# The numerators of a cached attention cross partitions by sixteen on-chip copies instead of by way of DRAM

## The chip, the cores and the metric

The kernel runs on one core of a Trainium2 chip. The metric is the device time of one execution in microseconds (us); lower is better. The five engines of the core work from queues of their own: TensorE (PE; its weight loads are PEld), VectorE (DVE), ScalarE (ACT), GpSimd (POOL) and SyncE (SP), which here issues nearly all DMAs. They wait for one another through semaphores.

## The reference, cut to what matters

One inference step of a small hybrid decoder: a recurrent layer, then a layer of "forgetting attention" in which each score carries a bias from a running sum of log forget values. It is done for a prompt of 2048 new tokens and, with the same weights, for 8 sample sequences of 8 new tokens each, which attend to 4096 cached positions in 32 pages of 128 rows. Model width 1024, 16 heads of 64.

```python
def fox_block(q, k, v, cq, ck, q_pos, k_pos):
    s = jnp.einsum('bqhd,bkhd->bhqk', q, k).astype(jnp.float32) * (HEAD_DIM ** -0.5)
    s = s + jnp.swapaxes(cq, 1, 2)[:, :, :, None] - jnp.swapaxes(ck, 1, 2)[:, :, None, :]
    mask = k_pos[None, :] <= q_pos[:, None]
    s = jnp.where(mask[None, None], s, -jnp.inf)
    p = jax.nn.softmax(s, axis=-1)
    return jnp.einsum('bhqk,bkhd->bqhd', p.astype(v.dtype), v)
...
    past_k = cache_k[page_table].reshape(Bs, past_len, N_HEADS, HEAD_DIM)
    past_v = cache_v[page_table].reshape(Bs, past_len, N_HEADS, HEAD_DIM)
```

All arithmetic is float32.

## The kernel before

The prompt's work (projections, the recurrence, the attention of 2048 tokens) is one long stream for TensorE. Beside it runs the cached attention of the samples, a generator `decode` that is advanced a step at a time. Its unit is a *turn*: one of 8 sequences and one of two groups of 8 heads, so 16 turns. Turns 0 and 1 run early, beside the first projections, one step after the other. Turns 2 to 15 run beside the second half of the projections and the prompt's attention, and there `period` overlaps three turns: the last products of the previous one, the softmax of this one and the scores of the next.

A turn goes like this:

- `pages` (L1074) loads the turn's 32 pages of keys, four pages of 256 KB into one tile `raw`; `V.transpose` (L1159) turns them into `ktr` in blocks of 32 by 32.
- `scores` (L1127) multiplies them with the queries. VectorE subtracts the result and the prefix sums `sc` of the log forget values from one another into `sc` (L106). `sc` is loaded once a turn from DRAM (L1116, 1 MB) and has one buffer. `new_scores` (L1142) does the same for the 8 new keys; both use one PSUM bank, `dS`.
- `softmax` finds the maxima, and ScalarE makes the numerators in `sc` in place. TensorE sums them (`dsum`, L1205).
- Eight transposes of blocks (L1212) bring the numerators to `sy`. They transpose within groups of 32 partitions only. What is still in the way is that the group of partitions (called i) and a block along the free axis (a) have to change places: 4 groups by 4 blocks, each 32 partitions by 512 values.
- This exchange goes through a DRAM scratch `pd`, one of two: four writes of 256 KB (L1217), one per group i, and one read of 1 MB into `sx` (L1218), which waits for the four writes. `sx` has one buffer; the turn's products read it until its end.
- `values` loads the 32 pages of values through the same four buffers of `raw`, and `products` (L1237) multiplies them with `sx` into `dO`. Then comes the result (L1265).

`sy` is taken from the buffers of `raw` in turns 2 to 15.

The order of the instructions on each engine is not written by hand alone: the program is built with a scheduler that plans all five engines from the dependences and its own estimates of durations, and the order that it finds is what the engines execute. A change of a few DMAs can move instructions everywhere behind it. On SP all DMAs stand in one line. In the compiled program they take eight semaphores in turn, and a DMA waits on its semaphore for the DMA eight before it to land (where another wait does not already make that sure), so that about eight are in flight.

Of the kernel before, what the change touches and what calls it, by code (L numbers as in the profile page):

```python
# [85 lines left out]
def tile_hawk_fox(  # L86
# [8 lines left out]
    V, A, G, T, S = nc.vector, nc.scalar, nc.gpsimd, nc.tensor, nc.sync  # L95
# [9 lines left out]
    def tt(eng, out, a, b, op):  # L105
        eng.tensor_tensor(out, a, b, op=op)  # L106
# [47 lines left out]
    def dt_(name, shape):  # L154
        return dram.tile(shape, F32, name=name, tag=name)
# [15 lines left out]
    qs_d = dt_("qsd", [DB, 32, 4, KB, DS])  # L171


    pd_d = [dt_(f"pd{i}", [4, 32, 4, 512]) for i in range(2)]

    c_d = dt_("cd", [2, 4, 4, DB, NPG // 4, 256])
    cn_d = dt_("cnd", [H, NSAMP])
# [846 lines left out]
    def decode(es, turns, nraw, nktr, ahead):  # L1024
# [28 lines left out]
        def bank(name, tag="d"):  # L1053
            return psum["dec"].tile([P, 512], F32, name=name, tag=tag, bufs=1)

        def spare():
            if ahead:
                return pool.tile([P, 2048], F32, name="sy", tag="raw", bufs=nraw)
            return pool.tile([P, 4096], F32, name="sy", tag="ktr", bufs=nktr)[:, :2048]

        def pages(cache, b, hg, g):

            with ExitStack() as order:

                if len(last) >= 3:
                    order.enter_context(tc.issue_after(last[-3]))
                regs = nc.values_load_multi_w_load_instructions(
                    pt1[0:1, b * NPG + g * 4:b * NPG + g * 4 + 4], engines=[SP], min_val=0, max_val=NPOOL - 1,
                    skip_runtime_bounds_check_because="the table was held between the first page and the last")[1]
            raw = pool.tile([P, 4, 512], F32, name="raw", tag="raw", bufs=nraw)  # L1070
            came = []
            for i in range(4):
                page = cache[ds(regs[i], 1), :, hg * 8:(hg + 1) * 8, :]
                d = S.dma_start(raw[:, i, :], page.rearrange("o k h d -> (o k) (h d)"))  # L1074
                came.append(d)
            last.append(d.ins)
            return raw, came
# [7 lines left out]
        def fetch_q(b):  # L1085
            qb = qbs[b] = pool.tile([P, 4, KB, DS], F32, name="qb", tag="qb")
            for a in range(4):
                S.dma_start(qb[a * 32:(a + 1) * 32], qs_d[b])

        def place_q(b, hg, pr):  # L1090

            G.tensor_tensor(  # L1092
                qw[:, pr].rearrange("p x (m q) -> p x m q", m=4),
                qbs[b][:, :, hg * 4 + pr, :].unsqueeze(2).to_broadcast([P, 4, 4, DS]),
                amask[:, :].unsqueeze(1).unsqueeze(3).to_broadcast([P, 4, 4, DS]), op=ALU.mult)
# [71 lines left out]
        def softmax(t):  # L1167

            dl = t.dl
            b, hg, gmx = t.b, t.hg, t.gmx  # L1170
            if not ahead:
                t.raws = [pages(cache_v, b, hg, x) for x in range(2)]
            while dl.q:
                dl.tick()
                yield HOP

            V.tensor_reduce(mx[:, :8], gmx[:, :, :].rearrange("p g h -> p h g"), axis=AX.X, op=ALU.max)
            mp = bank("dm")
            T.transpose(mp[:, :P], mx[:, :], ident[:, :])
            m1 = pool.tile([8, DS], F32, name="dm1", tag="dm1")  # L1180
            V.tensor_reduce(m1[:, :], mp[:8, :P].rearrange("h (a q) -> h q a", q=DS), axis=AX.X, op=ALU.max)
            V.tensor_scalar(mr[:8, :, :], m1[:, :].unsqueeze(1).to_broadcast([8, 16, DS]), -1.0, 0.0, op0=ALU.mult, op1=ALU.add)
            T.matmul(mp[:, P:P + 8], mr[:, :, :].rearrange("h a q -> h (a q)"), ident[:, :8], start=True, stop=True)
            nm = pool.tile([P, 8], F32, name="dnm", tag="dnm")
            V.tensor_copy(nm[:, :], mp[:, P:P + 8])
            if t.next and t.next[1] == 0:
                fetch_q(t.next[0])
            yield 3 * HOP

            ss = pool.tile([P, 2, 8], F32, name="dss", tag="dss")  # L1190
            tt(V, t.cn[:, :, :], t.cn[:, :, :], nm[:DS, :].unsqueeze(2).to_broadcast([DS, 8, DS]), ALU.add)
            A.activation(pn[:DS, :, :DS], t.cn[:, :, :], AF.Exp)
            V.tensor_reduce(ss[:DS, 1, :], pn[:DS, :, :DS], axis=AX.X, op=ALU.add)
            for j in range(4):
                for h in (2 * j, 2 * j + 1):
                    A.activation(t.sc[:, :, h, :], t.sc[:, :, h, :], AF.Exp, bias=nm[:, h:h + 1], accum_out=ss[:, 0, h:h + 1])
                if t.next:
                    place_q(*t.next, j)
                yield HOP
            tt(V, ss[:DS, 0, :], ss[:DS, 0, :], ss[:DS, 1, :], ALU.add)  # L1200
            dg = pool.tile([P, 8, DS], F32, name="ddg", tag="ddg")
            tt(V, dg[:, :, :], ss[:, 0, :].unsqueeze(2).to_broadcast([P, 8, DS]),
               qmask[:, :].unsqueeze(1).to_broadcast([P, 8, DS]), ALU.mult)
            sp = bank("dsum")
            T.matmul(sp[:, :64], ones[:, :], dg[:, :, :].rearrange("p h q -> p (h q)"), start=True, stop=True)  # L1205
            rb = t.rb = pool.tile([P, 64], F32, name="drb", tag="drb", bufs=2)
            V.reciprocal(rb[:, :], sp[:, :64])


            sy = spare()[:, :].rearrange("p (a x h q) -> p a x h q", a=4, x=8, h=8)  # L1210
            for h in range(8):
                V.transpose(sy[:, :, :, h, :].rearrange("p a x q -> p x a q"), t.sc[:, :, h, :])  # L1212

            sx = pool.tile([P, 4, 8, 8, DS], F32, name="sx", tag="sx")
            pd = pd_d[(b * 2 + hg) % 2]
            for i in range(4):
                S.dma_start(pd[:, :, i].rearrange("a l f -> l a f"), sy[i * 32:(i + 1) * 32].rearrange("p a x h q -> p a (x h q)"))  # L1217
            S.dma_start(sx[:, :, :, :, :].rearrange("p i x h q -> p (i x h q)"), pd.rearrange("a l i f -> (a l) (i f)"))  # L1218
            pt = pool.tile([32, 8, 32], F32, name="dpt", tag="dpt")
            V.transpose(pt[:, :, :].rearrange("p h x -> p (h x)"), pn[:, :, :].rearrange("p h x -> p (h x)"))  # L1220
            pc = t.pc = pcs[(b * 2 + hg) % 2]
            A.copy(pc[:32, :].rearrange("p (h q) -> p h q", h=8), pt[:, :, :DS])
            t.sx = sx
# [49 lines left out]
        def period(p, t, n):  # L1273


            chain_ = softmax(t)
            if n:
                begin(n)
            for who, x in (("v", 5), ("k", 0), ("v", 6), ("k", 1), ("v", 7), ("k", 2), ("k", 3), ("v", 0), ("k", 4),
                           ("v", 1), ("k", 5), ("v", 2), ("k", 6), ("v", 3), ("k", 7), ("v", 4)):  # L1280
                if (who, x) == ("v", 0):
                    yield from chain_
                if who == "k" and n:
                    yield from keys(n, [x])
                elif who == "v" and (t if x < 5 else p):
                    yield from values(t if x < 5 else p, [x])
                if x > 4 or who == "k" and x < 4:
                    yield from islice(chain_, 2)
# [7 lines left out]
        if ahead:  # L1296
            for p, t, n in zip([None] + ts, ts, ts[1:] + [None]):
                yield from period(p, t, n)
            yield from values(ts[-1], [5, 6, 7])
        else:  # L1300
            for t, n in zip(ts, ts[1:] + [None]):
                yield from softmax(t)
                yield from values(t, range(8))
                if n:
                    begin(n)
                    yield from keys(n, range(8))
# [532 lines left out]
```

## Time and profile before

| | |
|---|---|
| median of 3 runs | 3090.09 us (3083.68, 3090.09, 3090.77) |
| profiled execution, span | 3081.2 us (first to last instruction) |
| what lies around the span | 8.9 us, median less span; no time of its own is listed for the profiled execution |
| mean granted clock of TensorE | 0.965 |
| DMA packets, bytes | 492855, 653.25 MB |

The span of a profile runs from the first to the last instruction of one execution; the time of a run also has what the device does before and after. Names such as `sx<-pd` say what an instruction or DMA writes and reads, buffer numbers left out. A row of waits has the engine and line that waited, what ended the wait, the sum in us, the number of waits and the longest. A row in order of time has start, duration (of several merged instructions from the first to the last) and, where there is one, the idle time before in brackets. A row of a tile's instructions has their least, median and greatest duration in ns and the first and last start. A row of windows has the stretch, its length, busy us and instructions of PE, PEld, DVE, ACT and POOL, TensorE's granted clock, the DMA engines' share and GB/s.

### The profile page before, as it was taken

What the parts mean: (1) busy time and instruction counts of PE and PEld (TensorE: products, weight loads), DVE (VectorE), ACT (ScalarE), POOL (GpSimd) and SP (SyncE); (2) the same over time, 40 slices, a digit from 0 to 9 for tenths busy, and PEclk for the clock granted to TensorE, in tenths of its full rate; (3) what the DMA queues carried; (4) which work ended last, traced back from release to release, by engine and by line L of the source; (5) the groups of instructions that cost most, each with busy time, mean ns of one, the idle gap of its engine ahead of it and who ended that gap; (6) DMA issues with size and microseconds to landing.
All of it is one profiled execution on the core that took longest, in us unless ns stands there. A gap on an engine that the chain in (4) does not pass through costs nothing.

```text
span 3081.2 us, 58151 instructions
## 1 busy us (share of the span) xinstructions
PE 2825.8 (92%) x20462; PEld 2177.5 (71%) x20462; DVE 1805.6 (59%) x4012; ACT 1295.0 (42%) x2874; POOL 1155.5 (38%) x1263
## 2 busy tenths in 40 slices
PE   6998999998999989997999799899999988999798
PEld 5997888988999978885797455455545554544587
DVE  7876555424367756755655666666667665543244
ACT  4665432232346655333333334444444445455211
POOL 1663101000025532000001456655656648788322
PEclk9999999999999999998999799999999999999899
DMA  4224547788622266999999998989999996331343
GB/s 121 89 76 150 154 137 216 242 267 254 198 84 86 79 195 198 327 305 315 325 331 307 292 303 261 289 268 321 289 294 314 317 295 211 97 87 41 96 135 111
DMA packets 492855, 653.25 MB, mean 212 GB/s; under 512 B 91100, under 2 KB 292829, under 8 KB 485286
## 3 DMA queue, kind: packets, MB, share of 16 engines
q1 hardware_dynamic: 488934, 643.87, 66.9%
q10 hardware_dynamic: 3340, 3.56, 0.4%
q8 instruction: 162, 2.65, 0.4%
q0 software_dynamic: 288, 2.10, 0.2%
q14 instruction: 131, 1.07, 0.1%
HBM read 513.82 MB, written 135.16 MB: 211 GB/s over the span
## 4 chain that ended last, share of the span: by engine, by line
PE 54%; DMA 20%; DVE 10%; ACT 5%; SPq 5%; issue 4%; POOL 2%; ACTq 0%; DVEq 0%; POOLq 0%
PE ops L1557 5%; DMA raw<-in_cache_k_dram 5%; PE y L368 4%; PE y L370 4%; PE y L369 4%; PE st L1537 3%; DMA raw<-in_cache_v_dram 3%; PE kv L369 3%; PE kv L368 3%; PE kv L370 3%; PE sx L1404 3%; PE dO L1237 2%; SPq L1074 2%; PE qg L368 2%; PE st L1538 2%
## 5 line engine op out<-in xcount | busy, mean ns | idle before, releaser
L106 POOL TENSOR_TENSOR acc<-acc,p 128x512 f32<-128x512 f32 (+3 forms) x576 | 638.8, 1109 | 291.7 <-PE ops L1557 226.4
L1546 ACT ACTIVATE p<-st 128x512 f32<-128x512 f32 (+3 forms) x576 | 290.4, 525 | 404.8 <-PE st L1538 188.6
L1159 DVE STREAM_TRANSPOSE ktr<-raw 128x1024 f32<-128x1024 f32 x256 | 305.4, 1223 | 161.3 <-DMA raw<-in_cache_k_dram 143.7
L1406 DVE TENSOR_REDUCE mxs<-sx 128x1 f32<-128x512 f32 x384 | 253.9, 680 | 143.5 <-PE sx L1404 142.5
L369 PE MATMUL kv<-wl,xh 128*128 128x256 f32 (+3 forms) x1088 | 309.1, 287 | 8.9 <-DVE wl L413 8.8
L368 PE MATMUL kv<-wh,xh 128*128 128x256 f32 (+3 forms) x1088 | 310.4, 290 | 5.7 <-ACT wh L412 5.3
L370 PE MATMUL kv<-wh,xl 128*128 128x256 f32 (+3 forms) x1088 | 309.2, 286 | 0.0
L1557 PE MATMUL ops<-p,vvt 128*64 128x512 f32 (+3 forms) x1152 | 292.7, 550 | 3.1 <-ACT p L1546 2.8
L1537 PE MATMUL st<-qa,ka 128*128 128x512 f32 (+3 forms) x640 | 273.3, 427 | 21.8 <-ACT p L1546 18.0
L1404 PE MATMUL sx<-kbt,qbt 96*128 96x512 f32 (+3 forms) x640 | 234.7, 426 | 26.1 <-DMA qbt<-qd 11.5
L1537 PEld LDWEIGHTS st<-qa,ka 128*128 128x128 f32 x640 | 123.6, 193 | 178.5 <-issue 112.1
L412 ACT ACTIVATE wh<-wst,gv 128x256 fp32r<-128x256 f32 (+1 forms) x384 | 164.4, 499 | 195.0 <-DMA wst<-in_b_w_in_dram 81.8
L1538 PE MATMUL st<-qbt,kbt 128*128 128x512 f32 (+3 forms) x640 | 237.0, 371 | 0.0
L413 DVE SCALAR_TENSOR_TENSOR wl<-wst,gv,wh 128x256 fp32r<-128x256 f32 (+1 forms) x384 | 169.9, 492 | 108.1 <-ACT wh L412 100.3
L368 PE MATMUL qg<-xh,wh 128*128 128x384 f32 (+2 forms) x640 | 229.1, 359 | 1.0 <-ACT wh L412 1.0
L370 PE MATMUL qg<-xh,wl 128*128 128x384 f32 (+2 forms) x640 | 227.5, 357 | 0.9 <-DVE wl L413 0.9
L369 PE MATMUL qg<-xl,wh 128*128 128x512 f32 (+2 forms) x640 | 226.9, 356 | 0.0
L1092 POOL TENSOR_TENSOR qw<-qb,amask 128x128 f32<-128x128 f32 x64 | 29.3, 465 | 498.8 <-PE dS L1127 258.0
L369 PEld LDWEIGHTS kv<-wl,xh 128*128 128x128 f32 (+1 forms) x1088 | 203.8, 188 | 12.7 <-DVE wl L413 10.4
L368 PEld LDWEIGHTS kv<-wh,xh 128*128 128x128 f32 (+1 forms) x1088 | 203.6, 189 | 11.8 <-ACT wh L412 6.0
L370 PEld LDWEIGHTS kv<-wh,xl 128*128 128x128 f32 (+1 forms) x1088 | 205.3, 189 | 3.9 <-issue 3.9
L1404 PEld LDWEIGHTS sx<-kbt,qbt 96*128 96x128 f32 x640 | 119.1, 203 | 94.4 <-DVE mxs L1406 25.1
(289 smaller groups left out, 6472.1 us busy)
## 6 DMA issues: line engine op xcount, KB each, us to landing
raw<-in_cache_k_dram SPq DMA_DIRECT2D x512, 256.0 KB
raw<-in_cache_v_dram SPq DMA_DIRECT2D x512, 256.0 KB
wst<-in_w_kv_dram SPq DMA_DIRECT2D x48, 512.0 KB
wst<-in_b_w_in_dram SPq DMA_DIRECT2D x48, 512.0 KB
xt<-in_x_prompt_dram SPq DMA_DIRECT2D x32, 512.0 KB
wst<-in_a_w_in_dram SPq DMA_DIRECT2D x64, 256.0 KB
x<-x SPq DMA_DIRECT2D x32, 512.0 KB
out_dram<-kf SPq DMA_DIRECT2D x128, 128.0 KB
```

The lines of the kernel that those rows point to most:

```text
L106: eng.tensor_tensor(out, a, b, op=op)
L368: T.matmul(ps, lh(k), rh(k), start=(k == 0), stop=False)
L369: T.matmul(ps, lh(k), rl(k), start=False, stop=False)
L370: T.matmul(ps, ll(k), rh(k), start=False, stop=(k == nk - 1))
L413: V.scalar_tensor_tensor(wl[:, k, :], st[:, k, :], gk, f(wh[:, k, :]), op0=ALU.mult, op1=ALU.subtract)
L1159: V.transpose(t.kts[pp][:, n], raw[:, :, pp * 256:(pp + 1) * 256])
L1404: T.matmul(ps[:, :w], qb[0:96, j * P:(j + 1) * P], kb[0:96, ck * 512:ck * 512 + w], start=True, stop=True)
L1406: V.reduce_max(mx[:, j, ck:ck + 1], ps[:, :w], axis=AX.X)
L1537: T.matmul(ps[:, lo:], ka[:, ks], qa[:, lo:], start=True, stop=False)
L1538: T.matmul(ps[:, lo:], kb[:, ks], qb[:, lo:], start=False, stop=(k < qc * 4))
L1546: pair.append((k, lo, p, A.activation(p[:, lo:], ps[:, lo:], AF.Exp)))
L1557: return T.matmul(ops[r:r + HD, lo:], vvs[h % 2][:, k, :], p[:, lo:], start=(k < 2), stop=(last and k >= todo[-1][0] - 1))
```

## The change

The scratch `pd` is gone. The exchange is done by sixteen DMAs from `sy` to `sx`, one for each pair of a group i and a block a, each of 32 partitions by 512 values (64 KB). They stand at the same place in the generator, all on SP. The shapes of `sy` and `sx` and all that computes stay as they were. As the scratch is no longer there, lines behind it are numbered one lower in the changed program; this text uses the numbers of the kernel before, in which both kinds of copy stand at L1217.

```diff
-    pd_d = [dt_(f"pd{i}", [4, 32, 4, 512]) for i in range(2)]
...
             sx = pool.tile([P, 4, 8, 8, DS], F32, name="sx", tag="sx")
-            pd = pd_d[(b * 2 + hg) % 2]
             for i in range(4):
-                S.dma_start(pd[:, :, i].rearrange("a l f -> l a f"), sy[i * 32:(i + 1) * 32].rearrange("p a x h q -> p a (x h q)"))
-            S.dma_start(sx[:, :, :, :, :].rearrange("p i x h q -> p (i x h q)"), pd.rearrange("a l i f -> (a l) (i f)"))
+                for a in range(4):
+                    S.dma_start(sx[a * 32:(a + 1) * 32, i].rearrange("l x h q -> l (x h q)"),
+                                sy[i * 32:(i + 1) * 32, a].rearrange("l x h q -> l (x h q)"))
```

Every engine has the same instructions as before but SP, where 64 writes and 16 reads make way for 256 copies. Their order is the same on all engines up to the first exchange (turn 0) and is planned anew from there.

## The prediction

> **What bounds the kernel now.** I read the page first: the busy shares and the forty slices.
>
> ```profile
> span 3081.2 us, 58151 instructions
> PE 2825.8 (92%) x20462; PEld 2177.5 (71%) x20462; DVE 1805.6 (59%) x4012; ACT 1295.0 (42%) x2874; POOL 1155.5 (38%) x1263
> ...
> PE   6998999998999989997999799899999988999798
> ...
> DMA  4224547788622266999999998989999996331343
> ```
>
> TensorE is busy nearly everywhere, but from slice 17 to slice 33 the DMA engines stand at nine tenths as well. That is the stretch in which turns 2 to 15 of the cached attention run beside the prompt's work. So I asked for this stretch alone, then for what TensorE waits for in it, then for the chain that ended last in it.
>
> ```profile
> 1232.00:2480.00 1248.00, 1141.81 (x10175) 777.50 (x10173) 807.39 (x1628) 496.37 (x1230) 492.06 (x497) 0.95 0.96 304
> ```
>
> ```profile
> PE dO L1237 <- DMA raw<-in_cache_v_dram: 17.0, 13, 2.3
> PE dS L1142 <- DVE sc L106: 11.9, 6, 4.1
> PE dS L1127 <- DVE ktr L1159: 11.6, 4, 7.4
> PE sx L1404 <- DMA qbt<-qd: 11.5, 1, 11.5
> PE dO L1237 <- DMA sx<-pd: 6.8, 1, 6.8
> ```
>
> ```profile
> by line: DMA raw<-in_cache_k_dram 11.4%; PE ops L1557 6.5%; DMA raw<-in_cache_v_dram 6.0%; SPq L1074 5.2%; DMA sc<-cd 4.9%; issue 4.6%; PE dO L1237 4.4%; PE dS L1127 4.3%; PE st L1537 4.3%; PE sx L1404 3.7%; PE st L1538 2.9%; PE kv L369 2.7
> ```
>
> The first row says: of 1248.0 us TensorE is busy for 1141.8, so idle for 106.2; the DMA engines are busy for 0.96 of it and move 304 GB/s. The waits show that most of that idle time ends with a transfer or with VectorE work that a transfer released. The chain agrees: cached keys, cached values, SP's issue of them and the prefix sums `sc` make 11.4 + 6.0 + 5.2 + 4.9 = 27.5% of it. `sx<-pd` is not on that list. TensorE's work sets the end; the DMA engines, fed by one queue, decide how much idle time is added in this stretch.
>
> **The change, part by part.** These rows price the old path:
>
> ```profile
> L1217 SPq DMA_DIRECT2D pd<-sy x64: 302/431/2430, 628.4 to 2531.5; - x64
> L1218 SPq DMA_DIRECT2D sx<-pd x16: 319/430/1672, 635.0 to 2539.4; - x16
> ...
> PE dO L1237: 13.3, 3
> ```
>
> ```profile
> pd<-sy SPq DMA_DIRECT2D x64, 256.0 KB
> sx<-pd SPq DMA_DIRECT2D x16, 1024.0 KB
> ```
>
> ```profile
> 1326.07 3.49 SPq L1217 DMA_DIRECT2D pd<-sy  x4
> ...
> 1330.21 1.56 SPq L1116 DMA_DIRECT2D sc<-cd  x1
> ...
> 1334.85 2.00 SPq L1074 DMA_DIRECT2D raw<-in_cache_v_dram  x4
> 1339.14 0.33 SPq L1218 DMA_DIRECT2D sx<-pd  x1
> ```
>
> ```profile
> 1348.60 1.00 PE dO L1237 x16
> ```
>
> (The last row is the chain's, those before it are SP's in order of time.) In this turn the first write is issued at 1326.07, the read back at 1339.14, and the first product with `sx` runs at 1348.60: 22.5 us from start to use, with other loads and TensorE's other work between.
>
> *Removed: the wait on the second hop.* TensorE waited 13.3 us in three places for `sx<-pd` over the whole run (first fence). With one hop `sx` lands earlier by the 9 to 10 us that lie between the last write and the read's issue, against products that the new program puts no earlier: between the softmax's sum (L1205) and the turn's first product it has 147 TensorE instructions in the mean of turns 2 to 15, where the old one has 142. I take the whole 13 us off.
>
> *Removed: one megabyte a turn on the DMA engines.* At 304 GB/s the read of 1.05 MB costs 3.4 us, in fourteen turns 48 us of engine time.
>
> *Added: sixteen issues in a row where four stood.* No row shows a 64 KB copy between partitions. The nearest in kind are four 32 KB loads into 32 partitions each, and the four writes above:
>
> ```profile
> 2282.98 1.76 SPq L1088 DMA_DIRECT2D qb<-qsd  x4
> ```
>
> That is 0.44 us an issue when nothing holds SP, and 3.49 / 4 = 0.87 us when the queue is full, because each DMA of the program waits for the one eight before it. The train meets a full queue: its first eight copies go out at 0.87 us as the eight 256 KB transfers ahead of them land, its last eight at 0.44. That is 7.0 + 3.5 = 10.5 us. In that time the engines have 2.1 MB of backlog and 1.05 MB of copies to move, which is 10.3 us at 304 GB/s, so almost nothing is lost inside the train. After it only eight small copies (0.52 MB, 1.7 us) are in flight while SP issues pages again at 2.00 / 4 = 0.5 us, and I charge 2 us for filling up. The engines gain 3.4 - 2 = 1.4 us a turn, 20 us in fourteen turns. The bounds: if the train needs 0.87 us throughout, 16 x 0.87 = 13.9 us against 10.3 lose 3.6 more, and 3.4 - 2 - 3.6 = -2.2 us a turn, 31 us lost; if nothing is lost, 48 us gained. As DMA work and SP's issue of pages are some 28% of the chain there, I let a third of the 20 us through: 7 us off.
>
> The Trainium skill speaks against this part: in "DMA: Bandwidth & Descriptors", section "Rules for kernel authors", it asks that many small transfers be joined into large ones and says that under 64 KB one pays mostly overhead. By the 2.0 us per DMA that the page's section "Anatomy of one DMA" states (measured there on GpSimd's path), sixteen copies one after the other would cost some 34 us a turn as an estimate; eight at a time, some 4 us. This trace agrees only in part: its small loads go out every 0.44 us and overlap, so here issue time is what a small copy costs.
>
> *Moved: the load of the next turn's prefix sums.* It is queued behind the writes, and the next turn's scores wait for it:
>
> ```profile
> 1330.21 8.91 DMA sc<-cd
> ```
>
> ```profile
> 1339.21 0.69 DVE L106 TENSOR_TENSOR sc<-dS,sc 128x512 f32<-128x512 f32 x1 [3.29 <-DMA sc<-cd]
> ```
>
> (The first row is of the chain, the second of VectorE in order of time.) It is in transit for 8.91 us, and VectorE takes it 0.1 us after it lands. In the new program's order the train stands ahead of this load in eight of the thirteen turns that have a next one among 2 to 15, and behind it in five. In the eight it is issued 10.5 - 3.5 = 7 us later, but behind 0.52 MB instead of 2.1: 1.57 MB at 304 GB/s is 5.2 us, 3.7 less than 8.91. So it lands 3.3 us later, eight times 26 us in all; in the five it lands 3.5 us earlier, 17 us. What TensorE feels is another matter. The score product that needs the freed bank (L1142) stands 123 instructions behind the sum in the new order and 95 in the old. From the sum of turn 2 to the last product of turn 15 the old order has 6639 TensorE instructions, and these rows give their time:
>
> ```profile
> 1325.63 0.33 PE L1205 MATMUL dsum<-ddg,ones 128*128 128x64 f32 x2
> ```
>
> ```profile
> L1237 PE MATMUL dO<-raw,sx x2048: 376/379/637, 643.7 to 2572.4; 128*32 128x256 f32 x187
> ```
>
> 1246.8 us / 6639 = 0.19 us each, so 28 more instructions are 5.3 us more cover, more than the 3.3 us by which the load is late. Of the 11.9 us that TensorE waits there I take half off, 6 us; if the cover fails, the eight late loads add up to 26.
>
> *Moved: the end of the cached attention.* The whole order is planned anew, with the same instructions. The stretch of 6639 instructions has 6747 in the new program, while the prompt's attention ends at the same place. The same pages are spread over 108 x 0.19 = 20 us more of TensorE's work, which relieves the waits for keys and values (17.0 and 11.6 us). I book 3 us of it, and keep up to 20 for the range.
>
> *Added: a wait ahead of the train.* `sx` has one buffer, so the first copy waits until the previous turn's last product has read it. Before, only the late `sx<-pd` stood behind that. Queued behind it on SP are pages, prompt loads and, in eight turns, `sc`. In turn 4 that product came late:
>
> ```profile
> 1550.09 2.11 SPq L1217 DMA_DIRECT2D pd<-sy  x3
> ```
>
> ```profile
> 1556.57 1.07 PE L1237 MATMUL dO<-raw,sx 128*32 128x256 f32 x16
> ```
>
> There the copies would have stood for 1557.6 - 1550.1 = 7.5 us. The new order has the previous turn's last product clearly behind the sum in three turns, by 55, 24 and 20 instructions (10, 5 and 4 us). In all three the load of `sc` goes ahead of the train, and a full queue of eight is 7 us of work (2.1 MB at 304 GB/s), so little of it is idle time: 4 us added, 15 at worst.
>
> **The sum.** -13 - 7 - 6 - 3 + 4 = -25 us against the execution's own 3081.2 us span: 3056. The median of the runs, 3090.1, lies 8.9 us above that span, so 3065. The three terms of 7, 6 and 3 us each rest on the rows of one turn; I take 3 us off them together and forecast **3068 us**. The likeliest case's own range is 3050 to 3080: below, 18 us more from the spread and the engines; above, the uncertain gains gone.
>
> **The rivals.**
>
> *A, no difference (0.18).* The 13.3 us go, but the next transfer is late instead: DMA engines at 0.96 say that something always is, and `sx<-pd` is missing from the chain's list. The train gives back what the read costs. The waits for `sx` then return as waits for pages: 3081 to 3099, about 3088 us. Against it: the products' place in the order gains nothing, but the transfer gets 9 us.
>
> *B, slower: SP's train is the new bound (0.32).* All loads go through one queue. If a copy between partitions holds its place in the eight for longer than 0.44 us allows, the train lasts 13.9 us and not 10.5, and everything behind it (pages, `sc`, the prompt's `qbt` and `qa`) is 3.4 us later in each of fourteen turns. The point from which it decides is the 5.3 us of cover: 3.3 us of lateness fit, 6.7 do not, so about 1.4 us a turn show on the scores, 8 x 1.4 = 11 us, and the pages behind the train run dry for the 3.4 us, 48 us in all, of which I take half, 24; with the wait ahead of the train at its worst, 15, and 13 - 6 off for the hop and what replaces it: 11 + 24 + 15 - 7 = +43 at most and about +28 in its middle, 3118 us. For it: 65 us (5.2%) of the chain are already SP's issue of pages. Against it: four small loads in 1.76 us. The rule of the Trainium skill on small transfers, named above, points this way.
>
> *C, faster by more (0.10).* The stretch is bound by the DMA engines alone, and the 48 us of read come off nearly whole: 3042 to 3050 us. Against it: TensorE's idle time there is 106.2 us, and of the waits shown only 17.0 + 11.6 + 11.5 + 6.8 = 47 us end with a transfer or the transpose just behind one.
>
> **How the numbers follow.** About 0.3% (9 us) is what a measurement of this kernel can tell from no change. My forecast has 0.40, A 0.18, B 0.32, C 0.10. Faster by over 0.3%: 0.40 + 0.10 = 0.50; within: 0.18; slower: 0.32. The range reaches down over the likeliest case's own to 3046, into C, and up over A to 3120, past the middle of B; left out are half of C and the worse part of B, some 0.2.
>
> **What would show it.** Right, if in the profile of the changed kernel the sixteen copies of a turn take 9 to 12 us on SP; no TensorE wait names `sx<-sy`; the wait of L1142 on `sc` is under 11.9 us in the stretch; the DMA share there falls below 0.96 with about 15 MB less moved; and TensorE's idle time in it falls from 106 us to about 85. Wrong, if the train takes 14 us or more, if SP's own waits show the first copy standing for the previous turn's products (L1237) by more than 20 us in all, or if VectorE's wait for `sc<-cd` grows beyond the cover. Wrong too if the time moves in stretches that hold no cached attention: then the new order, not the copies, would be what counts.

## The result, and the profile after

The changed kernel takes 3121.98 us (median of 4 runs, 3121.08 to 3124.11), against 3088.0 for the kernel before on the same chip (4 runs, 3083.68 to 3090.77). The ratio is 1.0119, with a 95% interval of 1.0105 to 1.0132: slower by 1.2%. The forecast was 3068 us, its range ended at 3120. Rival B had said about 3118.

The page of the changed kernel, the rows that answer to those shown of before:

```profile
span 3119.3 us, 58366 instructions
PE 2838.6 (91%) x20462; PEld 2187.1 (70%) x20462; DVE 1801.9 (58%) x4012; ACT 1295.4 (42%) x2874; POOL 1154.2 (37%) x1263
...
DMA  3225447787622357999998988889889897431343
...
DMA packets 493623, 636.49 MB, mean 204 GB/s; under 512 B 93915, under 2 KB 295644, under 8 KB 488101
```

TensorE has the same 20462 instructions and is busy for 12.8 us more, at a mean granted clock of 0.958 instead of 0.965. The other 25 of the span's 38 us are idle time. The DMA engines move 16.8 MB less (653.25 before), as the change promised. But of the slices 17 to 33 only 9 still stand at nine tenths, where 15 of these 17 did.

The stretch of turns 2 to 15: the window, TensorE's waits in it, VectorE's wait for the prefix sums (sum, number, longest), and the chain:

```profile
1232.00:2480.00 1248.00, 1110.35 (x9698) 760.10 (x9700) 768.34 (x1543) 479.15 (x1179) 476.07 (x480) 0.93 0.90 282
```

```profile
PE dS L1141 <- DVE sy L1136: 19.9, 5, 9.0
PE dO L1236 <- DMA raw<-in_cache_v_dram: 17.8, 10, 3.3
...
PE kv L367 <- DMA xh<-xhd: 11.9, 1, 11.9
```

```profile
DVE sc L106 <- DMA sc<-cd: 31.1, 7, 6.8
```

```profile
by line: PE ops L1556 8.6%; DMA sc<-cd 6.5%; DMA raw<-in_cache_k_dram 5.6%; PE dO L1236 5.5%; PE st L1536 5.2%; PE dS L1126 4.9%; PE sx L1403 4.6%; issue 4.4%; DMA raw<-in_cache_v_dram 3.7%; PE st L1537 3.5%; SPq L1216 3.4%; PE kv L368 3.1%
```

In the same 1248 us TensorE gets through 9698 instructions instead of 10175, and its idle time is 137.7 us instead of 106.2. The DMA share falls from 0.96 to 0.90, and so does the rate, from 304 to 282 GB/s. Relief alone does not explain that: 1.05 MB less in each of fourteen turns, at the old pace, would be some 12 GB/s less, not 22, and the pace has fallen as well. The engines run dry. For `sx` TensorE waits 1.6 us in the whole run, instead of 13.3. VectorE's wait for the prefix sums has trebled; in the kernel before its row is

```profile
DVE sc L106 <- DMA sc<-cd: 10.5, 5, 4.4
```

SP's own issue of the copies (`SPq L1216`) is new on the chain.

SP in order of time, turn 2 (with the load of the prefix sums behind the train), a longer one of turn 5, and turn 6; below them the tile's row:

```profile
1320.60 11.93 SPq L1216 DMA_DIRECT2D sx<-sy  x16
1332.63 0.53 SPq L903 DMA_DIRECT2D out_dram<-kf  x1
1333.20 0.56 SPq L1115 DMA_DIRECT2D sc<-cd  x1
...
1678.75 14.40 SPq L1216 DMA_DIRECT2D sx<-sy  x16
...
1777.18 10.06 SPq L1216 DMA_DIRECT2D sx<-sy  x16
```

```profile
L1216 SPq DMA_DIRECT2D sx<-sy x256: 507/588/6422, 632.7 to 2619.5; - x128
```

An on-chip copy holds SP for 0.588 us in the median, where a write to `pd` held it for 0.431. The shortest train takes 10.06 us, which is 0.63 us an issue from the first to the last, with nothing in the way. For those 10 us SP issues 1 MB in all; the four writes of before took 3.49 in turn 2. Seven of the trains of turns 2 to 15 go out unbroken: they take 10.06 to 16.74 us, 13.6 in the mean, and four of them over 14.

How busy the DMA engines are while the exchange of turn 2 is issued, first in the changed kernel, then in the kernel before:

```profile
1320.60:1332.53 11.93, 10.53 (x138) 10.16 (x137) 9.02 (x14) 4.50 (x12) 0.00 (x0) 1.00 0.51 152
```

```profile
1326.07:1329.56 3.49, 3.49 (x32) 3.49 (x31) 2.44 (x3) 3.23 (x9) 0.00 (x0) 1.00 1.03 357
```

So they run dry inside the train already. 64 KB every 0.63 us is 104 GB/s, and the engines had been moving 304 in the stretch.

### The profile page after: what moved, and what is told of

Read it like the earlier page. It is cut to its first block, busy times and chain, and to the rows that moved or that the text cites. A ratio compares the mean times of both kernels' runs of the same rounds, so it can differ in the third digit from the quotient of the medians.

```text
span 3119.3 us, 58366 instructions
## 1 busy us (share of the span) xinstructions
PE 2838.6 (91%) x20462; PEld 2187.1 (70%) x20462; DVE 1801.9 (58%) x4012; ACT 1295.4 (42%) x2874; POOL 1154.2 (37%) x1263
## 4 chain that ended last, share of the span: by engine, by line
PE 55%; DMA 17%; DVE 9%; ACT 6%; SPq 6%; issue 4%; POOL 3%; ACTq 0%; DVEq 0%; POOLq 0%
PE ops L1556 6%; PE y L367 4%; PE y L368 4%; PE y L369 4%; DMA raw<-in_cache_k_dram 3%; PE st L1536 3%; DMA sc<-cd 3%; PE dO L1236 3%; PE kv L368 3%; PE kv L367 3%; PE kv L369 3%; PE sx L1403 3%; DMA raw<-in_cache_v_dram 2%; PE qg L367 2%; PE qg L368 2%
## 5 line engine op out<-in xcount | busy, mean ns | idle before, releaser
L367 PE MATMUL kv<-wh,xh 128*128 128x256 f32 (+3 forms) x1088 | 310.7, 289 | 17.4 <-DMA xh<-xhd 11.9
L367 PE MATMUL qg<-xh,wh 128*128 128x512 f32 (+2 forms) x640 | 229.4, 359 | 0.0
L367 PEld LDWEIGHTS kv<-wh,xh 128*128 128x128 f32 (+1 forms) x1088 | 204.0, 189 | 23.1 <-DMA xh<-xhd 12.1
```

What stands on the lines that cost most here:

```text
L367: T.matmul(ps, lh(k), rh(k), start=(k == 0), stop=False)
```

## The experiments

All ratios are against the kernel before, run on the same chip (its median lay between 3077 and 3083 us). Line numbers in rows are those of each program.

**First round: which part of the train costs?** The theory was that the number of issues on SP costs, by their time and by their places in the line of DMAs (theory 1). Rivals were the late load of `sc`, the on-chip kind of copy, SP as the issuer, and the new order that the scheduler plans. In this round and the next the scheduler planned each kernel anew.

*order_only*: the kernel before with four scratches instead of two.

```diff
-    pd_d = [dt_(f"pd{i}", [4, 32, 4, 512]) for i in range(2)]
+    pd_d = [dt_(f"pd{i}", [4, 32, 4, 512]) for i in range(4)]
...
-            pd = pd_d[(b * 2 + hg) % 2]
+            pd = pd_d[(b * 2 + hg) % 4]
```

> The kernel before with four DRAM scratches in turn where it had two: the same copies, the same instructions, but the planner gives the engines another order from early on. Theory 1 (SP's train: the sixteen on-chip copies hold SP about 0.63 us each, everything behind them in the one line of DMAs is late and the DMA engines run dry): no change that matters, 3079 to 3098 us. Theory 2 (the new order itself costs the time, the copies are innocent): a shift of 20 us or more, to either side, is as likely as none.

Measured: 3082.46 us, ratio 1.0002 (0.9984 to 1.0019). It tells nothing of the order: instruction by instruction the program stands in exactly the order of the kernel before. The premise of this run was wrong, and I first read it as clearing the order.

*writes16*: the kernel before with sixteen writes of 64 KB to DRAM, and the read back.

```diff
-                S.dma_start(pd[:, :, i].rearrange("a l f -> l a f"), sy[i * 32:(i + 1) * 32].rearrange("p a x h q -> p a (x h q)"))
+                for a in range(4):
+                    S.dma_start(pd[a, :, i], sy[i * 32:(i + 1) * 32, a].rearrange("p x h q -> p (x h q)"))
```

> The kernel before with the four writes of 256 KB to the DRAM scratch cut into sixteen of 64 KB; the read of 1 MB stays. So many issues as the change has, but none from partitions to partitions. Theory 1, if the number of issues is what counts: a train of 16 x 0.47 = 7.5 us instead of 3.5, a third to a half of the change's loss: 3098 to 3112 us. Theory 1, if the kind counts (an on-chip copy holds SP 0.63 us, a write less): 3085 to 3098. Theory 2: no relation to either.

Measured: 3128.13 us, ratio 1.0143 (1.0120 to 1.0166). With an order of its own, sixteen small DMAs cost as much without being on-chip copies.

*act_queue* and *pool_queue*: the changed kernel with the copies issued by ScalarE, and by GpSimd.

```diff
-                    S.dma_start(sx[a * 32:(a + 1) * 32, i]...
+                    A.dma_start(sx[a * 32:(a + 1) * 32, i]...      # act_queue
+                    G.dma_start(sx[a * 32:(a + 1) * 32, i]...      # pool_queue
```

> The changed kernel with all sixteen copies issued by ScalarE's queue in place of SP's. Theory 1: SP is free for pages, the loss is gone unless ScalarE suffers from some 10 us of issuing a turn: 3060 to 3095 us, and DMA share in the stretch back at 0.95 or above. Theory 2: about 3120 still, or anywhere.

> The changed kernel with all sixteen copies issued by GpSimd's queue. Theory 1: SP's line is free again, GpSimd is busy for 38% only: 3070 to 3100 us if its issues take about 1 us each and its adds can wait. If what the copies do to the DMA engines were the cost, and not SP's time: 3115 or more. ScalarE's queue gave 3176 as ScalarE stood behind the train; the same would show here as waits of GpSimd's adds, and then more than 3130.

Measured: 3176.51 us, ratio 1.0306 (1.0283 to 1.0329), and 3178.39 us, ratio 1.0328 (1.0280 to 1.0377). Both are worse than the change. ScalarE's queue in order of time and a wait of ScalarE in act_queue:

```profile
1322.33 22.11 ACTq L1216 DMA_DIRECT2D sx<-sy  x16
```

```profile
ACT p L1545 <- DMA sx<-sy: 52.4, 13, 8.9
```

The train shown takes 22 us, and the prompt's exponentials stand behind it. In pool_queue TensorE waits for pages of values instead:

```profile
PE dO L1236 <- DMA raw<-in_cache_v_dram: 64.8, 22, 8.7
```

TensorE is also busy for longer there, 2882.9 us instead of 2825.8; why is not shown. Another issuer is no way out in these two runs. The Trainium skill, "DMA: Bandwidth & Descriptors", section "Issuing engines are not separate DMA queues", says that it only saves the sequencer's time, and calls that time usually small beside the transfer. No run here shows the first half by itself. The second does not fit this case: 64 KB at 304 GB/s are 0.2 us of the DMA engines' time, and the issue holds SP for 0.588.

*copies32* and *copies12*: thirty-two copies of 32 KB; and twelve copies of 64 KB, the four from a group to itself done by VectorE.

```diff
-                    S.dma_start(sx[a * 32:(a + 1) * 32, i]..., sy[i * 32:(i + 1) * 32, a]...)
+                    for e in range(2):                                                # copies32
+                        S.dma_start(sx[a * 32:(a + 1) * 32, i, e * 4:(e + 1) * 4]..., sy[i * 32:(i + 1) * 32, a, e * 4:(e + 1) * 4]...)
...
+                    (V.tensor_copy if a == i else S.dma_start)(...)                   # copies12
```

> The changed kernel with thirty-two copies of 32 KB a turn in place of sixteen of 64 KB: the same bytes, twice the issues. Theory 1: a train of 32 x 0.63 = 20 us or more, ten more a turn; if half of that is seen in the end as it was with the first ten, 3150 to 3190 us. Theory 2: about 3120, give or take 20, as the bytes are the same and the order is again another.

> The changed kernel with the four copies that stay in their own group of partitions (i = a) done by VectorE right behind its transposes, so twelve DMAs a turn in place of sixteen. Theory 1 (SP's train; 11 more issues than before cost some 37 us, 27 more some 75): seven more, about 24 us, 3100 to 3113 us. Against it, a cost that hangs on copies between partitions being there at all, or on the new order: about 3120 still.

Measured: 3154.04 us, ratio 1.0251 (1.0212 to 1.0290), and 3116.99 us, ratio 1.0129 (1.0081 to 1.0177). Twice the number costs about twice as much, at the same bytes; three quarters of it are no cheaper than the whole, which theory 1 did not expect.

*sc_first* and *sc_first_dram*: six empty steps in the generator between the transposes and the exchange, so that the load of `sc` goes ahead of the exchange in all thirteen turns; in the changed kernel and in the kernel before.

```diff
                 V.transpose(sy[:, :, :, h, :]...
+            if ahead:
+                for _ in range(6):
+                    yield 0.0
             sx = pool.tile([P, 4, 8, 8, DS], F32, name="sx", tag="sx")
```

> The changed kernel, in turns 2 to 15 with the sixteen copies put behind the load of the next turn's prefix sums by six empty steps of the generator; the line then has that load ahead of the train in all thirteen turns, not in five. Two parts of theory 1 (SP's train) are told apart. 1a, the late prefix sums are what TensorE feels: half of the loss or more comes back, 3092 to 3108 us. 1b, all loads behind the train are late and the engines run dry, whichever comes first: 3113 to 3130 us.

> The kernel before with the same six empty steps: the four writes go behind the load of the prefix sums, which is then issued some 3.5 us earlier. 1a: a gain, 3055 to 3076 us, if the products can wait for a later read back. 1b: no change that matters, 3078 to 3098 us.

Measured: 3152.93 us, ratio 1.0245 (1.0197 to 1.0293), and 3075.88 us, ratio 0.9987 (0.9960 to 1.0014). TensorE's longest wait in sc_first:

```profile
PE dO L1239 <- DMA raw<-in_cache_v_dram: 69.4, 20, 8.9
```

What is put ahead of the train is on time, and what is behind it is late: pages of values instead of `sc`. As far as runs with orders of their own can tell, the late load of `sc` is a symptom. In sc_first_dram the place made no difference that can be told from none.

Of theory 1's ranges in this round only that of copies32 was met in a run that could test it; writes16, act_queue, pool_queue, copies12 and sc_first all came out above theirs.

**Second round: number or bytes?**

*copies4*, *copies1* and *quarter_bytes*: four on-chip copies of 256 KB, one of 1 MB, and sixteen of 16 KB. The first two leave out the exchange between the groups of partitions, the third three quarters of the numerators from the second turn on (its products read the quarter again); they serve to measure only.

```diff
-                for a in range(4):
-                    S.dma_start(sx[a * 32:(a + 1) * 32, i]..., sy[i * 32:(i + 1) * 32, a]...)
+                S.dma_start(sx[:, i]..., sy[:, i]...)                                  # copies4
...
+            S.dma_start(sx[:, :, :, :, :]..., sy[:, :, :, :, :]...)                    # copies1
...
+                nx = 2 if b + hg else 8                                                # quarter_bytes
+                for a in range(4):
+                    S.dma_start(sx[a * 32:(a + 1) * 32, i, :nx]..., sy[i * 32:(i + 1) * 32, a, :nx]...)
```

> The changed kernel with four on-chip copies of 256 KB a turn (128 partitions, each onto itself) in place of sixteen of 64 KB: the same bytes, the same kind, the same single hop. The exchange between the four groups of partitions is left out. Theory 1 (each small copy holds SyncE for 0.63 us and takes one of the places in the line of DMAs, the engines run dry behind it): four issues hold SyncE about 2.5 us, the DMA share of turns 2 to 15 goes back to 0.95 or more with 1 MB a turn less than before, a turn takes 90 to 93 us; 3050 to 3085 us, no slower than before. Rival (on-chip copies as such are slow for the DMA engines, or the single hop brings an order that is worse): 98 us a turn, 3105 to 3125 us.

> The same with one on-chip copy of 1 MB a turn (the exchange between the groups is left out again). Theory 1: as with four copies, 3045 to 3085 us; the issue holds SyncE about 0.6 to 2.5 us. If the last step from four to one is worth more than 5 us, one issue is worth about 0.2 us a turn and the sixteen are linear in count (12 issues x 13 turns x 0.2 = 31 us). Rival: 3105 to 3125 us.

> The changed kernel with sixteen copies of 16 KB a turn from the second turn on: as many issues, a quarter of the bytes (the other three quarters of the exchanged numerators are left out, and the products read the quarter again). Theory 1: the issues hold SyncE as long as with 64 KB (0.6 us each, 10 us a train and more), the turn stays at 95 to 99 us, 3100 to 3125 us, although a turn moves 1.5 MB less by the engines' count. Rival (the bytes of on-chip copies are what the DMA engines are slow at): the turn falls to 91 to 93 us, 3060 to 3085 us.

*no_dma*: the exchange by VectorE and ScalarE, with a step of the generator behind each group's four copies.

```diff
-                    S.dma_start(sx[a * 32:(a + 1) * 32, i]...
+                    (A.copy if a % 2 else V.tensor_copy)(sx[a * 32:(a + 1) * 32, i]...
...
+                yield 0.0
```

> The exchange without any DMA: sixteen copies of 32 partitions x 512 numbers from group to group by VectorE (eight) and ScalarE (eight), some 0.42 to 0.5 us each, about 4 us on each engine beside one another. Nothing left out. Theory 1: no issue on SyncE, no place in the line, and 1 MB a turn less written and read than the changed kernel: a turn of 86 to 92 us, 3030 to 3075 us, faster than both kernels. Rival (what the change lost lies in the scheduled order of SyncE's and VectorE's work around the exchange, or VectorE is short of time in these turns: 768 us busy of 1248): 3085 to 3125 us.

Measured: copies4 3101.33 us, ratio 1.0077 (1.0055 to 1.0099); copies1 3074.51, 0.9995 (0.9975 to 1.0015); quarter_bytes 3153.87, 1.0226 (1.0197 to 1.0256); no_dma 3103.2, 1.0065 (1.0040 to 1.0090). A quarter of the bytes is no faster, which speaks against the bytes as the price. But theory 1 missed three of the four. Four copies should have been no slower than before, no copies at all should have won, and quarter_bytes lies 29 us above its range. Each of these kernels has another planned order, so number and order were mixed in every run so far.

**Third round: the order held.** These programs are built twice. The first build gives the planned order of one kernel; in the second every instruction of every engine, SP's other DMAs included, is tied to its predecessor in that order, and the scheduler places only the exchange. In the traces the instructions outside the exchange do stand in that order.

```diff
+        for k in order:                 # places in the order of the first build, the exchange left out
+            i, e = ins[k], str(ins[k].engine)
+            if e in last:
+                tc.add_manual_dep(i, last[e].name, NoSync, reason="order")
+            last[e] = i
```

So there are four corners: either exchange in either order. *copies_old_order* has the change in the order of before, *dram_new_order* the DRAM path in the order of the change.

> The sixteen copies with the order of the kernel before: every instruction of every engine, SyncE's other DMAs too, stands in exactly the order of the kernel before; the copies alone are put in by the scheduler (whole trains of sixteen, seven of the thirteen behind the load of the prefix sums). Theory 1 (the copies themselves cost: each holds SyncE 0.6 us and a place in the line of DMAs): 3100 to 3125 us, a turn of 96 to 99 us. Theory 2 (the order that the scheduler plans around the copies costs, the copies do not): 3055 to 3085 us, the gain of the prediction.

> The writes to DRAM and the read back, with the order of the changed kernel: every other instruction of every engine stands as in the changed kernel. Theory 1: 3075 to 3095 us, as the kernel before. Theory 2: 3110 to 3130 us, as the changed kernel. If copies_old_order and this one both lie between, copies and order share the 38 us, and the two differences give the shares.

*copies4_old_order* has the copies of copies4 (the exchange between the groups is left out again), and *no_dma_old_order* those of no_dma, in the order of before.

> Four on-chip copies of 256 KB a turn, each group of partitions onto itself (the exchange between the groups is left out), with the order of the kernel before on all engines. Theory 1 (number of issues): 3050 to 3080 us, 25 us and more under copies_old_order. Theory 2 (order): the same as copies_old_order within 10 us. With the order planned anew it took 3101.

> The exchange by VectorE and ScalarE (eight copies each a turn, no DMA), with the order of the kernel before on all engines; the sixteen copies are put in by the scheduler. Nothing left out. With the order planned anew it took 3103. Theory 1: nothing on SyncE, 2 MB a turn less for the DMA engines: 3030 to 3070 us. Theory 2: the 3103 came from the planned order; here 3040 to 3075 us as well. Rival to both (VectorE's 3.4 us and ScalarE's 4 us a turn lie on the path from the softmax to the products and ahead of the transposes of keys): 3085 to 3110 us.

Measured:

| exchange | order of before | order of the change |
|---|---|---|
| by DRAM | 1 (before) | 1.0101 (1.0071 to 1.0131), 3109.45 us |
| sixteen copies | 1.0314 (1.0290 to 1.0339), 3173.55 us | 1.0119 (1.0105 to 1.0132) |
| four copies | 0.9911 (0.9891 to 0.9932), 3053.91 us | not tried |
| no DMA, VectorE and ScalarE | 1.0003 (0.9984 to 1.0021), 3075.85 us | not tried |

In the order of before the sixteen copies cost 3.1%, some 97 us (their place has moved a little: before, all thirteen loads of `sc` stood behind the writes, here eight stand ahead of the train), and four copies of the same bytes gain 0.9%. The two differ in 12 issues a turn, 192 in sixteen turns, and in 119.6 us: 0.62 us an issue in the mean of all turns. The windows, TensorE's waits and SP in order of time, first of copies_old_order:

```profile
1232.00:2480.00 1248.00, 1082.64 (x9511) 750.41 (x9510) 751.10 (x1508) 460.80 (x1141) 440.06 (x449) 0.92 0.89 276
```

```profile
PE dS L1142 <- DVE sc L106: 41.8, 7, 7.7
PE dO L1251 <- DMA raw<-in_cache_v_dram: 36.7, 11, 12.7
```

```profile
1325.84 11.41 SPq L1231 DMA_DIRECT2D sx<-sy  x16
1337.35 0.52 SPq L904 DMA_DIRECT2D out_dram<-kf  x1
1337.92 0.57 SPq L1116 DMA_DIRECT2D sc<-cd  x1
```

and then the same of copies4_old_order:

```profile
1232.00:2480.00 1248.00, 1154.49 (x10320) 784.19 (x10319) 815.53 (x1636) 502.43 (x1245) 508.78 (x514) 0.95 0.95 298
```

```profile
PE dO L1251 <- DMA raw<-in_cache_v_dram: 19.2, 13, 3.2
...
PE dS L1142 <- DVE sc L106: 9.3, 5, 3.2
```

```profile
1317.21 2.51 SPq L1227 DMA_DIRECT2D sx<-sy  x4
1319.81 0.84 SPq L904 DMA_DIRECT2D out_dram<-kf  x1
1320.70 0.69 SPq L1116 DMA_DIRECT2D sc<-cd  x1
```

Bytes and order are the same, and both kinds of copy stay on the chip; in fifteen of the sixteen turns the trains also stand at the same places among SP's other DMAs. What differs besides the number is that the four copies have 128 partitions each and the sixteen 32. With sixteen issues `sc` is issued 12.1 us after the train began, with four 3.5 us. The wait of L1142 for it goes from 9.3 to 41.8 us, that for pages of values from 19.2 to 36.7, and the DMA engines move 276 GB/s instead of 298. Of the 113.7 us between the two spans 95.0 are idle time of TensorE and 18.7 its longer busy time. That is theory 1 at a held order, though by its range copies_old_order was to take 3125 us at most and took 49 more. Of its two parts, SP's time and the places in the line of DMAs, the trace of the changed kernel favours the first: in the shortest train a copy has landed 2.0 us after its issue began, so that in that train about three are in flight and not eight. A run that parts the two was not made. That 0.62 us an issue comes so near to the 0.63 of that train is partly chance: unbroken trains of turns 2 to 15 took 13.3 us in the mean with sixteen issues and 3.4 with four, so longer by 9.9 and not by 7.5.

The second column is what I had not reckoned with. In the planned order of the change the DRAM path is slower too, by 31 us, and with the copies it is hardly slower than that (1.0119 against 1.0101, intervals that overlap):

```profile
1232.00:2480.00 1248.00, 1133.52 (x9966) 780.09 (x9968) 786.63 (x1607) 495.85 (x1215) 485.65 (x502) 0.94 0.94 298
```

(dram_new_order, windows.) The new order, planned with the train in it, takes some 60 us of the 97 away again. But it is an order that gets through 9966 instructions in the stretch where the old one got through 10175. So the 1.2% of the change, 37 us by the ratio, can be split in two ways, and both are measured: 97 for the copies less 60 for the order planned with them, or 31 for the order and 6 for the copies in it (which by the intervals may be nothing). Which instructions of the new order cost the 31 us stays open.

**A version that beats both?** The bytes are worth having. no_dma_old_order makes the exchange in full without a DMA, yet gains nothing over before, a miss too (theory 1 had 3070 us at most). Its tile rows and TensorE's waits:

```profile
L1223 DVE COPY sx<-sy x128: 371/418/1415, 628.7 to 2524.1; 32x512 f32<-32x512 f32 x128
L1223 ACT COPY sx<-sy x128: 613/617/623, 630.4 to 2525.5; 32x512 f32<-32x512 f32 x128
```

```profile
PE st L1551 <- ACT p L1560: 14.3, 15, 4.5
...
PE sx L1418 <- DVE mxs L1420: 12.5, 10, 5.5
```

In the kernel before these two waits are

```profile
PE st L1537 <- ACT p L1546: 6.6, 13, 1.6
PE sx L1404 <- DVE mxs L1406: 5.6, 9, 1.3
```

TensorE now waits about twice as long for ScalarE's `p` and VectorE's `mxs`, so I took ScalarE out, and then VectorE too, in the same order.

```diff
-                        exch((A.copy if a % 2 else V.tensor_copy)(sx[...
+                        exch((G.tensor_copy if a % 2 else V.tensor_copy)(sx[...       # vector_gpsimd
+                        exch(G.tensor_copy(sx[...                                     # gpsimd_alone
```

> As no_dma_old_order, with GpSimd in the place of ScalarE: eight copies by VectorE and eight by GpSimd a turn, the order of the kernel before on all engines. Nothing left out. There TensorE's waits for ScalarE's exponentials rose by some 20 us over the kernel before (p of L1546: 20.8 and 11.2 us in the stretch), because a copy holds ScalarE for 0.617 us. Theory (the gain of the bytes, 23 us with copies4_old_order, was eaten by the engines that make the copies): 3055 to 3070 us. Rival (any engine's copies cost as much, by VectorE's share alone): 3072 to 3090 us.

> All sixteen copies by GpSimd, the order of the kernel before on all engines. Nothing left out. GpSimd has 482 us of work in the 1248 us of the stretch; a copy takes an estimated 0.55 us (1072 ns for 128 x 1024, halved), 9 us a turn, and the products have 22 us from the transposes to their first use. Theory: neither VectorE's nor ScalarE's work is delayed; 3050 to 3070 us. Rival (GpSimd's sums for the prompt's attention stand behind the copies, and TensorE waits for the buffers that they free): 3080 to 3100 us.

Measured: vector_gpsimd 3090.16 us, ratio 1.0043 (1.0022 to 1.0063), a miss; gpsimd_alone 3068.15 us, ratio 0.9983 (0.9963 to 1.0003). The latter has the lowest ratio of the kernels with the whole exchange. By these ratios it beats the changed kernel by 1.4% (0.9983 against 1.0119); from the kernel before and from sc_first_dram it cannot be told. So none beats both. The tile rows of vector_gpsimd, then that of gpsimd_alone:

```profile
L1223 DVE COPY sx<-sy x128: 372/737/1420, 627.3 to 2533.3; 32x512 f32<-32x512 f32 x128
L1223 POOL COPY sx<-sy x128: 603/694/869, 627.4 to 2533.8; 32x512 f32<-32x512 f32 x128
```

```profile
L1223 POOL COPY sx<-sy x256: 599/607/857, 629.5 to 2518.4; 32x512 f32<-32x512 f32 x128
```

## Why the prediction was wrong, step by step

**Removed: the second hop, and a megabyte a turn. Right.** 13 and 7 us were booked. copies4_old_order has these two, with one issue a turn fewer, and is 23 us under the kernel before; the runs do not separate them. In the changed kernel 1.6 us of waits for `sx` are left, and 16.8 MB are gone.

**Added: sixteen issues. This is the step that failed.** Two things in it were wrong. The durations came from DMAs with one end in DRAM: 0.44 us an issue with a free queue and 0.87 with a full one. An on-chip copy takes 0.63 us with a free queue, so my 10.5 us hit the shortest train (10.06) by two errors that cancel; the mean of the unbroken ones is 13.6. The larger error came after: "almost nothing is lost inside the train", because the engines have a backlog, and so 1.4 us a turn gained, of which a third counts. In turn 2, on whose rows I had built this, the DMA engines' share was 0.51 while the train was issued, and 1.03 while the four writes were. Nor did only a third come through: at a held order 12 issues a turn cost 119.6 us, 7.5 a turn, about as much as 12 issues of 0.63 take with nothing in the way (7.6). And what stands behind the train is needed soon: in the stretch the waits for `sc` (L1142) and for pages of values grew by 32.5 and 17.5 us. The bound on this term was 31 us lost; at the held order copies instead of DRAM lost 97.

**Moved: the load of `sc`. The cover failed.** I took 6 us off and named 26 if it fails. At the held order the wait of L1142 rose by 30 (11.9 to 41.8 us). In the changed kernel, where the order has the cover that I counted, TensorE waits instead for `sy` of L1136 (19.9 us) while VectorE's wait for `sc` trebles. sc_first tried one other place for the train, and there the pages of values behind it were late.

**Moved: the end of the cached attention. Not borne out.** I took the longer spread of the same pages as relief, 3 us with up to 20. The order with that spread costs 31 us with the old exchange in it; what the spread alone does stays open. I had counted instructions between two points, and not asked what the order had been planned for.

**Added: the wait for the previous products. Harmless**, as its low end: SP's waits in the changed kernel have

```profile
SPq L1216 <- PE dO L1236: 1.0, 1, 1.0
```

**Rival B** had the right time, 3118, and the right mechanism: a copy that holds its place longer than 0.44 us, with `sc` and pages late behind it. Its train of 13.9 us is near the mean of 13.6. It was not right in size: it had +43 us at most, and at the held order the copies cost 97. That the end result still fell at 3122 is because the order planned with the train took 60 of these away; the prediction had no case for that, so B's time is partly luck.

**The signs that I named** were ambiguous. A DMA share under 0.96 with 15 MB less was to mean right; it came, and meant engines run dry. So did the L1142 wait on `sc` under 11.9 us, which is 4.7 in the changed kernel. TensorE's idle time (137.7 us, not 85) did tell, and so did trains of over 14 us and VectorE's longer wait for `sc`. The time did not move ahead of the stretch: in the first 1232 us TensorE gets through 7684 instructions, before 7663.

## What to carry to other kernels

Where one queue issues all loads and the engines behind it are nine tenths busy, count a DMA by the time for which it holds the issuer, and let all of it through to the end; its bytes come second. Look up that time for the very kind of copy, and read a falling DMA share only together with the idle time of the engine that sets the end. And where a scheduler plans the order, an edit is two edits: hold the order of the old kernel to see what the edit costs, and put the old code into the new order to see what the order costs.

## What the runs showed of the hardware

An on-chip copy holds SP for 0.588 us in the median (0.515 when ScalarE issues it and 0.498 on GpSimd, in act_queue and pool_queue), a copy of 16 KB for 0.588 (quarter_bytes) and one of 256 KB for 0.593 (copies4_old_order), so size hardly matters; a write to DRAM of the same data held it for 0.431.

A VectorE copy of 32 x 512 takes 418 ns beside ScalarE's copies and 737 ns beside GpSimd's, GpSimd's 694 instead of 607 when alone. The Trainium skill, "GPSIMD Engine Reference", section "1. Specifications", says that GpSimd's way into on-chip memory is shared with VectorE and contended by VectorE's instructions in a two-port mode or with two on-chip inputs; the longer times agree, but no run shows whether this copy is one of those.

TensorE's granted clock was lower in every clearly slower kernel: 0.953 in copies_old_order and 0.958 in the changed kernel, against 0.965 before and 0.966 in copies4_old_order. The same 20462 instructions took 2844.4, 2838.6, 2825.8 and 2825.7 us:

```profile
PE 2844.4 (90%) x20462; PEld 2193.2 (69%) x20462; DVE 1804.2 (57%) x4012; ACT 1295.8 (41%) x2874; POOL 1155.1 (36%) x1263
```

```profile
PE 2825.7 (92%) x20462; PEld 2179.0 (71%) x20462; DVE 1804.4 (59%) x4012; ACT 1294.4 (42%) x2874; POOL 1154.0 (38%) x1263
```

(The pages of copies_old_order and copies4_old_order.) One place shows how. TensorE in order of time in copies_old_order, and windows around it:

```profile
1461.90 2.15 PE L1251 MATMUL dO<-raw,sx 128*32 128x256 f32 x16 [12.68 <-DMA raw<-in_cache_v_dram]
```

```profile
1461.90:1466.00 4.10, 3.55 (x48) 3.16 (x48) 1.13 (x3) 0.00 (x0) 0.00 (x0) 0.50 1.03 296
1466.00:1470.00 4.00, 3.75 (x66) 3.17 (x66) 0.21 (x1) 0.00 (x0) 0.00 (x0) 0.57 1.14 284
1470.00:1476.00 6.00, 6.00 (x51) 5.96 (x48) 1.55 (x3) 0.38 (x1) 0.00 (x0) 1.00 1.12 304
```

After 12.68 us of waiting for a page the clock granted is 0.50, and it is whole again some 8 us later (in the 9 us ahead of the wait it was 0.81). So a long wait costs more than its length. The Trainium skill, "TensorE: Matmul & The Clock Gate", section "HAM oscillation — how this bites in real kernels", asks for no idle gap of over some 3.4 us for this reason; the trace agrees. Counted in the traces, without the wait for its first instruction, TensorE has 26 such gaps in copies_old_order, 17 in the changed kernel, 13 in the kernel before and 9 in copies4_old_order, the order of their clocks. The number alone does not set the clock: writes16 has 16 and a clock of 0.954.
